# A 64-byte side load from sixteen rows, and the engine that waits for the last store, in a multiply-and-GELU kernel

## The chip, the cores and the metric

The kernel runs on one core of one Trainium2 chip. The metric is the device time of one execution in microseconds. Four executions of the kernel before took 119.97, 120.05, 120.23 and 120.64 us, with a median of 120.14 us. The profile shown here is that of the execution that took 119.97 us.

## The reference

Two float32 arrays `x` and `y` of 1024 x 4096 are multiplied element by element, and the tanh form of GELU is applied to the product.

```python
z = x * y
return (0.5 * z * (1 + np.tanh(np.sqrt(2 / np.pi) * (z + 0.044715 * z ** 3)))).astype(np.float32)
```

Each array has 16.78 MB. Two are read and one is written, so 50.33 MB cross between HBM and the on-chip memory (SBUF) in any version that reads and writes each element once.

## The kernel before

The arrays are seen as flat and cut into three pieces. A piece spans a range of columns of a picture of 128 partitions by 32768 columns: columns 0 to 1280 (640 KB in all), 1280 to 17664 (8 MB) and 17664 to 32768 (7552 KB). Inside a piece, each partition's columns are one contiguous run in HBM, and the partitions follow one another. A row below is one partition's part of a piece: 5 KB, 64 KB or 59 KB. Here the pieces are called the first, the second and the third.

All of `x` has a place in SBUF (`xs`), and the results are written over it. `y` has a smaller buffer (`ys`, 20440 columns), so its third and first pieces go where the second was, after parts of that have been used. `Y_LOADS` lists the pieces of `y` in the order of their loading, second, third, first, with their places in `ys`; `Y_FREE` says how many multiplications must be done before each load may be issued (0, 3 and 4).

All loads and stores are issued by SyncE (SP in the profile), in an order written out by hand:

1. `x` first piece and `x` second piece. `_hoist` moves these two issues ahead of the barrier among the engines with which the program begins.
2. After the barrier, `y` second piece and `x` third piece.
3. `y` third piece, after three multiplications, and `y` first piece, after four.
4. The three stores (line 113), second, third, first, each after the GELU of its columns (line 112).

VectorE multiplies (line 96) in steps of 4096 columns for the second piece, of 2048 and 768 for the third, and of 1280 for the first. ScalarE (ACT) applies GELU to each step (line 104) once `sem_mul` says that it is multiplied. At the end SyncE waits for the first two stores (line 115) and clears the semaphores but one (line 118). ScalarE waits for the last store and takes that semaphore back to zero (line 119):

```python
nc.sync.sem_clear(range(nums[0], nums[-1] + 1))
nc.scalar.wait_ge(sem_o[-1], 16).then_inc(sem_o[-1], -16)
```

ScalarE issues no transfer in this version. Line 59 is the closing of the tile scheduler, in which the engines pass two more rounds of the barrier.

Of the kernel before, what the change touches and what calls it, by code (L numbers as in the profile page):

```python
# [1 line left out]

# [4 lines left out]


F32 = mybir.dt.float32
GELU = mybir.ActivationFunctionType.Gelu_apprx_tanh  # L10

PIECES = [(0, 1280), (1280, 17664), (17664, 32768)]

Y_LOADS = [(1280, 17664, 4056), (17664, 32768, 0), (0, 1280, 15104)]

Y_FREE = [0, 3, 4]

STEPS = [[4096] * 4, [2048] * 7 + [768], [1280]]  # L20
STORES = [(1280, 17664), (17664, 32768), (0, 1280)]
Y_BUF = 20440


def _hoist(nc, issued):

    here = nc.cur_bb.bb.instructions
    first = nc.main_func.blocks[0].instructions
    for ins in issued:
        del here[next(k for k, i in enumerate(here) if i is ins or i.name == ins.name)]  # L30
    engine = issued[0].engine
    at = next(
        k
        for k, i in enumerate(first)
        if i.engine == engine and type(i).__name__ == "InstDrain"
    )
    first[at:at] = issued


@with_exitstack  # L40
def kernel(
    ctx: ExitStack,
    tc: tile.TileContext,
    x: bass.AP,
    y: bass.AP,
    out: bass.AP,
):
    nc = tc.nc
    P = nc.NUM_PARTITIONS

    def columns(t, a, b):

        flat = t.flatten_outer_dims().rearrange("r c -> (r c)")
        pa, pb = next(q for q in PIECES if q[0] <= a and b <= q[1])
        return flat[P * pa : P * pb].rearrange("(p c) -> p c", p=P)[:, a - pa : b - pa]


    tc.close()
    tc.compile()  # L59

    xs = nc.alloc_sbuf_tensor("xs", [P, PIECES[-1][1]], F32).ap()
    ys = nc.alloc_sbuf_tensor("ys", [P, Y_BUF], F32).ap()
    sem_x = [nc.alloc_semaphore(f"sem_x{i}") for i in range(len(PIECES))]
    sem_y = [nc.alloc_semaphore(f"sem_y{i}") for i in range(len(Y_LOADS))]
    sem_mul = nc.alloc_semaphore("sem_mul")
    sem_act = nc.alloc_semaphore("sem_act")
    sem_o = [nc.alloc_semaphore(f"sem_o{i}") for i in range(len(STORES))]

    def load_x(i):
        a, b = PIECES[i]  # L70
        return nc.sync.dma_start(out=xs[:, a:b], in_=columns(x, a, b)).then_inc(sem_x[i], 16)

    def load_y(i):
        a, b, r = Y_LOADS[i]
        return nc.sync.dma_start(
            out=ys[:, r : r + b - a], in_=columns(y, a, b)
        ).then_inc(sem_y[i], 16)

    _hoist(nc, [load_x(0).ins, load_x(1).ins])
    load_y(0)  # L80
    load_x(2)
    for i in range(1, len(Y_LOADS)):
        if Y_FREE[i]:
            nc.sync.wait_ge(sem_mul, Y_FREE[i])
        load_y(i)

    n = 0
    done = {}
    for i, (a, b, r) in enumerate(Y_LOADS):
        for j, (xa, xb) in enumerate(PIECES):  # L90
            if xa <= a < xb:
                nc.vector.wait_ge(sem_x[j], 16)
        nc.vector.wait_ge(sem_y[i], 16)  # L93
        c = a
        for w in STEPS[i]:
            nc.vector.tensor_mul(  # L96
                out=xs[:, c : c + w],
                in0=xs[:, c : c + w],
                in1=ys[:, r + c - a : r + c - a + w],
            ).then_inc(sem_mul, 1)  # L100
            n += 1
            done[c + w] = n
            nc.scalar.wait_ge(sem_mul, n)
            nc.scalar.activation(  # L104
                out=xs[:, c : c + w], in_=xs[:, c : c + w], func=GELU
            ).then_inc(sem_act, 1)
            c += w

    for i, (a, b) in enumerate(STORES):
        if i == 0:  # L110
            nc.sync.wait_ge(sem_y[-2], 16)
        nc.sync.wait_ge(sem_act, done[b])
        nc.sync.dma_start(out=columns(out, a, b), in_=xs[:, a:b]).then_inc(sem_o[i], 16)
    for i in range(len(STORES) - 1):
        nc.sync.wait_ge(sem_o[i], 16)
    nums = sorted(s.num for s in [*sem_x, *sem_y, *sem_o[:-1], sem_mul, sem_act])
    assert nums == list(range(nums[0], nums[-1] + 1))
    nc.sync.sem_clear(range(nums[0], nums[-1] + 1))
    nc.scalar.wait_ge(sem_o[-1], 16).then_inc(sem_o[-1], -16)


# [1 line left out]
_INS = ['x', 'y']  # L123
_OUTS = [((1024, 4096), 'float32')]


# [23 lines left out]
```

## Time and profile before

| What | Value |
|---|---|
| Time, median of four executions | 120.14 us (119.97 to 120.64) |
| Time of the profiled execution | 119.97 us |
| Its span, from the first to the last instruction of the program | 118.5 us |
| Time outside the span | about 1.5 us |
| Bytes moved, mean rate over the span | 50.33 MB, 425 GB/s |
| VectorE busy | 35.2 us (30% of the span) |
| ScalarE busy | 31.0 us (26%) |
| Share of the 16 DMA engines taken by packets | 98.8% |

The span begins with the first issue of a transfer on SyncE and ends with ScalarE's wait for the last store. The profile names an engine's queue of instructions with a q: SPq is SyncE issuing or waiting. An issue has a start, a length (the time SyncE spends on it), and a time to landing, counted from its start until the last of its bytes is reported. A landing in the span is the sum of the two. The table of windows gives busy time and transfers in stretches of the span that the reader of the trace chooses.

### The profile page before, as it was taken

The page shows a single profiled execution, that of the slowest core. Times are in us where ns is not written, and L with a number is a line of the kernel's source. Part 1 is how long each engine was busy: PE and PEld are TensorE (multiplying, and loading weights), DVE is VectorE, ACT ScalarE, POOL GpSimd, SP SyncE. Part 2 cuts the span into 40 slices and gives each one's busy share as a digit, 9 for nine tenths or more (in the row PEclk, how much of TensorE's full clock was granted, in tenths as well). Part 3 has the DMA queues.
Part 4 walks back from the last instruction along what each step waited for, and adds up shares of the span by engine and source line. Part 5 has one row for each costly group of instructions (what it writes and reads, how often), then busy time and mean ns, then how long its engine had stood idle before and what let it go on. Part 6 is the DMA issues. An engine that isn't in the chain of part 4 may idle for free.

```text
span 118.5 us, 82 instructions
## 1 busy us (share of the span) xinstructions
DVE 35.2 (30%) x13; ACT 31.0 (26%) x14; POOL 0.2 (0%) x4
## 2 busy tenths in 40 slices
DVE  0000000000000069999920000059999940000000
ACT  3000000000000001977974000006998990000000
POOL 0000000000000000000000000000000000000000
DMA  7988899888988897797797798798899887977975
GB/s 260 669 354 354 354 620 443 354 354 376 686 354 354 354 653 326 326 653 326 326 632 347 326 632 347 326 575 354 354 553 509 354 354 326 653 326 326 653 326 221
DMA packets 1296, 50.33 MB, mean 425 GB/s; under 512 B 144, under 2 KB 144, under 8 KB 528
## 3 DMA queue, kind: packets, MB, share of 16 engines
q1 hardware_dynamic: 1296, 50.33, 98.8%
HBM read 33.55 MB, written 16.78 MB: 425 GB/s over the span
## 4 chain that ended last, share of the span: by engine, by line
DMA 53%; DVE 24%; ACT 3%; issue 1%; DVEq 0%
DMA ys<-in_y_dram 53%; DVE xs L96 24%; ACT xs L104 3%; DVEq L93 0%
## 5 line engine op out<-in xcount | busy, mean ns | idle before, releaser
L96 DVE TENSOR_TENSOR xs<-xs,ys 128x2048 f32<-128x2048 f32 (+3 forms) x13 | 35.2, 2777 | 60.9 <-DMA ys<-in_y_dram 60.9
L104 ACT ACTIVATE xs<-xs 128x2048 f32<-128x2048 f32 (+3 forms) x13 | 29.7, 2301 | 64.7 <-DVE xs L96 64.7
L104 ACT ACT_TABLE_LOAD x1 | 1.3, 1283 | 1.9 <-PEq L59 1.9
L134 POOL MEMSET const-bfloat16-1.0<- 128x1 bf16 x1 | 0.1, 101 | 0.0
L134 POOL MEMSET const-uint8-127<- 128x1 uint8 x1 | 0.1, 101 | 0.0
L134 POOL MEMSET const-float32-0.0<- 128x1 f32 x1 | 0.1, 98 | 0.2 <-issue 0.2
L134 POOL MEMSET const-float32-1.0<- 128x1 f32 x1 | 0.1, 98 | 0.0
## 6 DMA issues: line engine op xcount, KB each, us to landing
xs<-in_x_dram SPq DMA_DIRECT2D x1, 7552.0 KB, 58.1
ys<-in_y_dram SPq DMA_DIRECT2D x1, 7552.0 KB, 22.5
out_dram<-xs SPq DMA_DIRECT2D x1, 7552.0 KB, 20.4
xs<-in_x_dram SPq DMA_DIRECT2D x1, 640.0 KB, 3.6
ys<-in_y_dram SPq DMA_DIRECT2D x1, 640.0 KB, 19.7
out_dram<-xs SPq DMA_DIRECT2D x1, 640.0 KB, 20.8
xs<-in_x_dram SPq DMA_DIRECT2D x1, 22.7
ys<-in_y_dram SPq DMA_DIRECT2D x1, 40.5
```

The source lines that it names most:

```text
L96: nc.vector.tensor_mul(out=xs[:, c : c + w], in0=xs[:, c : c + w], in1=ys[:, r + c - a : r + c - a + w],).then_inc(sem_mul, 1)
L104: nc.scalar.activation(out=xs[:, c : c + w], in_=xs[:, c : c + w], func=GELU).then_inc(sem_act, 1)
L134: nc = _bacc.Bacc("TRN2", target_bir_lowering=False, num_devices=1)
```

## The change

There are two edits.

The first adds a small load, called `touch`. ScalarE issues it, ahead of the first barrier. It reads 16 columns (64 B) of every eighth row of the second piece of `x`, sixteen rows in all, and writes them into `ys[:16, :16]`. These columns of `ys` are not used by the second piece of `y`; the third piece of `y` is loaded over them later. Nothing computes with the bytes. The load has a semaphore of its own, `sem_t`, and SyncE waits for it between the issue of the third piece of `x` and that of the third piece of `y`. `sem_t` is added to the range that is cleared at the end.

The second edit moves the wait for the last store from ScalarE to SyncE, behind SyncE's clearing of the other semaphores.

```diff
+    sem_t = nc.alloc_semaphore("sem_t")
...
+    a = PIECES[1][0]
+    touch = nc.scalar.dma_start(out=ys[:16, :16], in_=columns(x, a, a + 16)[:: P // 16, :]).then_inc(sem_t, 16)
+    _hoist(nc, [touch.ins])
     _hoist(nc, [load_x(0).ins, load_x(1).ins])
     load_y(0)
     load_x(2)
+    nc.sync.wait_ge(sem_t, 16)
     for i in range(1, len(Y_LOADS)):
...
-    nums = sorted(s.num for s in [*sem_x, *sem_y, *sem_o[:-1], sem_mul, sem_act])
+    nums = sorted(s.num for s in [sem_t, *sem_x, *sem_y, *sem_o[:-1], sem_mul, sem_act])
     assert nums == list(range(nums[0], nums[-1] + 1))
     nc.sync.sem_clear(range(nums[0], nums[-1] + 1))
-    nc.scalar.wait_ge(sem_o[-1], 16).then_inc(sem_o[-1], -16)
+    nc.sync.wait_ge(sem_o[-1], 16).then_inc(sem_o[-1], -16)
```

On every engine the other instructions stand in the same order as before.

## The prediction

> **What bounds the kernel now.** I read the page's queue line first, then its table of issues, then a table of windows cut at the landings, and last the waits of SyncE.
>
> ```profile
> DVE 35.2 (30%) x13; ACT 31.0 (26%) x14; POOL 0.2 (0%) x4
> q1 hardware_dynamic: 1296, 50.33, 98.8%
> DMA 53%; DVE 24%; ACT 3%; issue 1%; DVEq 0%
> ```
>
> Packets take 98.8% of the 16 DMA engines' time, and no compute engine is busy for a third of the span. The chain (third line) credits VectorE with 24%, but that is the order in which the last store was released; the queue stayed full meanwhile. So the end is set by the transfers, back to back from the first to the last, and an edit counts only if it starts the stream later, opens a hole in it, lengthens it, or lengthens what follows it.
>
> ```profile
> 0.00 0.38 SPq L71 DMA_DIRECT2D xs<-in_x_dram  x1
> 0.43 0.42 SPq L71 DMA_DIRECT2D xs<-in_x_dram  x1
> xs<-in_x_dram SPq DMA_DIRECT2D x1, 640.0 KB, 3.6
> xs<-in_x_dram SPq DMA_DIRECT2D x1, 22.7
> ```
>
> These are two rows of the timeline (start, length) and two of the issue table (size, time to landing). The first x piece is issued at 0.00 and lands at 3.6; the second at 0.43 and lands at 0.43 + 22.7 = 23.1. Doing the same for every issue gives the cuts of this table of windows; its first two columns are the stretch and its length.
>
> ```profile
> 0.00:3.63 3.63, 0.00 (x0) 1.28 (x1) 0.20 (x4) 1.00 1.23 469
> 3.63:23.10 19.47, 0.00 (x0) 0.00 (x0) 0.00 (x0) 1.00 1.00 431
> 23.10:42.45 19.35, 0.00 (x0) 0.00 (x0) 0.00 (x0) 1.00 0.99 429
> 78.20:79.74 1.54, 1.45 (x1) 0.00 (x0) 0.00 (x0) 1.00 2.14 910
> 79.74:99.10 19.36, 16.33 (x9) 15.26 (x9) 0.00 (x0) 1.00 0.99 429
> ```
>
> The rows are: x first piece, x second, y second, y first, store of the second. I use their lengths only (the last two columns, DMA share and GB/s, jump in a short stretch). Two comparisons matter. The second piece is 8 MB in three of the rows: x took 19.47 us, y 19.35, its store 19.36. So beside its equals the second x piece has lost only 0.11 to 0.12 us, and that is all that the small load can give back there. The first piece of 640 KB took 3.63 us at the start and 1.54 in the stream, for y: a start from nothing costs 2.09 us. A further window, 0.50 to 1.00, shows 0 GB/s, and 1.00 to 1.50 the first 174, so about 1.0 us of that is the way from issue to first packet, and 1.09 us is slow first rows and landing.
>
> **The small load, on its engine.** ScalarE gains one issue before the first barrier. SyncE's issues last 0.33 to 0.53 us, the nearest rows. ScalarE's other work there is a barrier drain at 0.1 us; SyncE reaches the barrier only after its two hoisted issues (0.85 us) and its drain at 0.9. If ScalarE issues from about 0.1, it is done by 0.1 + 0.53 = 0.63 and is not last at the barrier: cost 0. Without that cover the barrier would be late by the issue's length, and with it the y issue at 1.91. That too is covered: the y bytes are wanted only at 23.1. ScalarE's table load (1.92, 1.28 us) is wanted at 47.01, when its first GELU starts. So a late barrier costs nothing up to some 20 us.
>
> **The small load, in the transfers.** It adds 1 KB, sixteen packets of 64 B, probably one on each DMA engine, and 16 semaphore increments. The nearest row is the 640 KB piece in the stream: 1.54 us for 128 rows on 16 engines, so 8 rows on each at 0.19 us. A 64 B packet costs its engine between 0 (it fits into the slow first rows) and 0.19. I take half, 0.10, since the streaming row carries 80 times the bytes, but this packet is the first of its kind, and the first rows here are slow. The issue could also delay that of the first x piece, if the two cannot be served together: 0 to 0.42 us, from the length of SyncE's second hoisted issue. I take 0, since SyncE starts first and its own first issue is over at 0.38, where ScalarE has hardly begun.
>
> The Trainium skill has a rule that speaks against the edit: by "DMA: Bandwidth & Descriptors", section "Issuing engines are not separate DMA queues", transfers issued from several engines interleave on the same 16 DMA engines, so that a second issuer saves issue time alone; and its section "Measured (HBM→SBUF, 128 partitions, SWDGE, issued from GpSimd)" puts 4 KB at 0.68 us of transfer. If all of that stood ahead of the first x piece, an estimate by the page would be 119.97 + 0.68 = 120.65 us in the profiled execution. The page's figure is for another way of issuing, and no row here shows a transfer of this size, so it is no end of my range.
>
> **What it may give.** It reads from sixteen rows of the second x piece about two microseconds before that piece's turn. If that piece's deficit is the price of a first access, up to 0.11 us comes back. Against this stands the row of y: its second piece is just as untouched at 23.1 and shows no such loss. The stores' row agrees with y. So the 0.11 may as well be left from the disturbed start. The bounds are -0.11 and 0; I take -0.05, halfway.
>
> **The new wait on SyncE.** Behind `wait_ge(sem_t)` are queued the third and first pieces of y, and then the stores. The wait starts when the third x piece is issued, 2.29 + 0.53 = 2.82 us. The touch would land near the first x piece, at 3.6.
>
> ```profile
> 55.68 4.66 SPq L75 DMA_DIRECT2D ys<-in_y_dram  x2
> SPq L75 <- DVE xs L96: 56.8, 2, 52.8
> ```
>
> The next issue behind it is at 55.68 in the timeline, after 52.8 us of waiting for the third multiplication, as SyncE's waits say. A touch that lands at 3.6, or at 20, is hidden. Cost 0, cover some 50 us. The third y piece is stored over the touched columns after that wait, so no transfer is moved.
>
> **The last wait.** Before, SyncE waits for the second store at 116.9 and clears at 117.0; ScalarE's wait ends the span at 118.5. After, SyncE clears at the same point and then waits, so the clear stays hidden under the last store's 1.5 us, and one more semaphore in the range adds nothing. The wait is one instruction of 17 ns on either engine. What differs is what follows it outside the span, 119.97 - 118.5 = 1.5 us that no view of this trace divides by engine. The nearest row is a round of the barrier at the start:
>
> ```profile
> SPq L59 <- PEq L59: 0.5, 2, 0.3
> ```
>
> SyncE waits twice there, 0.3 us the longest. If the end is a round of the same kind, a late SyncE in place of a late ScalarE can shift it by up to one round, 0.3 us either way. Nothing excludes either sign; I take 0.
>
> **The sum.** 119.97 + 0.10 (packets) - 0.05 (second x piece) + 0 (issue, barrier, wait on `sem_t`) + 0 (last wait) = 120.02 us. The median of the four runs is 0.17 above the profiled one, so the forecast is 120.19, given as 120.2. A difference of 0.5%, 0.60 us, is about what a measurement of this kernel can tell from no change: below 119.54 is faster, above 120.74 slower. My terms taken together at their ends, -0.11 - 0.3 = -0.41 and +0.19 + 0.42 + 0.3 = +0.91, give 119.73 to 121.05.
>
> **Rivals.** *The touch pays the first transfer's start, and the first x piece queues behind it* (slower). The place is the first 3.6 us. The price is anything up to the 1.09 us that the 640 KB piece loses there beside its equal, on top of the way to the first packet; it decides the verdict once over half of it, 0.60 us, comes on top of what the first piece pays already. Then the first landing moves from 3.6 to between 4.2 and 4.7 and the time is 120.7 to 121.2. For it: every DMA engine would carry the small packet, and nothing in the stream can make up a late start. Against it: SyncE issues first, and two cold reads may wait side by side. Chance 0.26.
>
> *The touch and the moved wait both help* (faster). The deficit of 0.11 goes, the end gains 0.3, and the first piece itself finds a warmer path, gaining up to half of its 1.09: 120.14 - 0.11 - 0.3 - 0.55 = 119.2. Less than a gain of 0.2 in the first piece leaves it inside 0.60. For it: the first rows are slow. Against it: the touch reads other rows than the first piece's, and is issued later. Chance 0.12.
>
> *The touch warms nothing*, because what the second x piece loses is not a first access: 120.14 + 0.10 = 120.24, inside the forecast's case, which has 0.62 in all.
>
> **The numbers.** Faster 0.12, same 0.62, slower 0.26. For the range I take 119.6 to 121.0: it holds the forecast's case, from its low end of 119.73 and a little into the faster rival, and most of the slower one. Left out are about 0.10 below and 0.08 above.
>
> **What would show it.** Right: the first x piece still lands at 3.6 to 3.8 and the second between 23.0 and 23.2; stages of 8 MB at 19.35; SyncE's issue at 55.68 moves by no more than that; SyncE's last wait ends the span at 118.4 to 118.7; 1.5 us, give or take 0.3, remain outside. Wrong: a first landing after 4.2; a second x piece that gains more than 0.11; a hole in a later stage; or a time outside the span that differs by more than 0.3 us, for which the ScalarE queue or the place of the last wait would have to answer.

## The result: 0.15% less time, from the end of the program

The changed kernel takes 119.78 us (median of 46 runs, 119.67 to 121.12); beside it, the kernel before took 119.98 us (76 runs, 119.74 to 120.64). The ratio is 0.9985, with a 95% interval of 0.9979 to 0.9991. That is 0.18 us less. It is inside the 0.5% that the prediction called no change, and clear of no change all the same, thanks to the number of runs. The forecast was 0.05 us more than before. So the time lies in the stated range, and the direction was the other one.

The profiled execution after took 119.81 us, with the same span of 118.5 us as before. So 1.3 us instead of 1.5 stand outside the span. Over the 47 runs after whose span is listed, time less span has a mean of 1.34 us. For the kernel before it was 1.51, 1.49 and 1.52 in the three groups of runs in which it was measured beside the experiments. (Spans are listed to 0.1 us; the means smooth that.)

The page after, first the engines, then the queues, then the chain:

```profile
DVE 35.2 (30%) x13; ACT 31.0 (26%) x14; POOL 0.2 (0%) x4
q1 hardware_dynamic: 1296, 50.33, 98.6%
q10 hardware_dynamic: 32, 0.00, 0.0%
DMA 53%; DVE 24%; ACT 3%; issue 1%; DVEq 0%; SPq 0%
```

New are q10, and `SPq` at 0% in the chain (a wait at line 89 that is now an instruction of its own). q10 is ScalarE's queue: 32 packets, the 16 of the touch and their 16 semaphore increments. A share that prints as 0.0% is below 0.05% of 16 engines' 118.5 us, which is 0.95 us over all of them, or less than 0.06 us on each.

The timeline at the start after:

```profile
0.12 0.38 ACTq L81 DMA_DIRECT2D ys<-in_x_dram  x1
0.42 0.42 SPq L72 DMA_DIRECT2D xs<-in_x_dram  x1
1.91 0.33 SPq L76 DMA_DIRECT2D ys<-in_y_dram  x1
1.91 1.28 ACT L109 ACT_TABLE_LOAD   x1 [1.91 <-PEq L59]
```

Two rows of its issue table (size, time to landing):

```profile
xs<-in_x_dram SPq DMA_DIRECT2D x1, 640.0 KB, 3.5
ys<-in_x_dram ACTq DMA_DIRECT2D x1, 1.0 KB, 3.0
```

ScalarE's issue lasts 0.38 us and is over at 0.50. The first issue behind the barrier stands at 1.91, as before. The touch lands at 0.12 + 3.0 = 3.1, and the first x piece at 3.5 instead of 3.6.

The windows after, cut at the landings as in the prediction:

```profile
0.00:3.53 3.53, 0.00 (x0) 1.28 (x1) 0.20 (x4) 1.00 1.21 483
3.53:23.19 19.66, 0.00 (x0) 0.00 (x0) 0.00 (x0) 1.00 0.99 427
23.19:42.53 19.34, 0.00 (x0) 0.00 (x0) 0.00 (x0) 1.00 0.99 430
78.20:79.77 1.57, 1.47 (x1) 0.00 (x0) 0.00 (x0) 1.00 2.03 864
79.77:99.14 19.37, 16.30 (x9) 15.26 (x9) 0.00 (x0) 1.00 0.99 429
```

The second x piece, the one whose rows were touched, now takes 19.66 us instead of 19.47. The y piece and the store of the same size take 19.34 and 19.37. So the second row is longer, not shorter; the first row is 0.10 shorter, and both together end at 23.19 instead of 23.10. Where one transfer ends and the next begins varies by itself: in six profiles without the touch, with the same loads up to there, the first x piece landed between 3.38 and 3.63 us and the second took 19.45 to 19.75 us. Inside the span there is no gain to be found.

Two of SyncE's waits after:

```profile
SPq L89 <- DVE xs L101: 52.9, 1, 52.9
SPq L124 <- SPq L124: 1.4, 1, 1.4
```

The last instruction of the span, from the trace's answers on its line, before and after (duration in ns, start in us):

```profile
L119 ACTq EVENT_SEMAPHORE  x1: 17/17/17, 118.5 to 118.5; - x1
L124 SPq EVENT_SEMAPHORE  x1: 17/17/17, 118.5 to 118.5; - x1
```

Line 124 is the wait that moved. It lasts 1.4 us behind the clearing and ends the span at 118.5, as ScalarE's did. The releaser is given as its own line, presumably since the wait also takes the semaphore back.

### The profile page after: what moved, and what is told of

Read it like the earlier page. It is cut to its first block, busy times and chain, and to the rows that moved or that the text cites. A ratio compares the mean times of both kernels' runs of the same rounds, so it can differ in the third digit from the quotient of the medians.

```text
span 118.5 us, 84 instructions
## 1 busy us (share of the span) xinstructions
DVE 35.2 (30%) x13; ACT 31.0 (26%) x14; POOL 0.2 (0%) x4
## 4 chain that ended last, share of the span: by engine, by line
DMA 53%; DVE 24%; ACT 3%; issue 1%; DVEq 0%; SPq 0%
DMA ys<-in_y_dram 53%; DVE xs L101 24%; ACT xs L109 3%; DVEq L98 0%; SPq L89 0%
```

## The experiments

Two theories stood against each other. By the end theory, the gain lies behind the last instruction and comes from the engine that waits last. By the touch theory, it lies in the first 23 us and comes from the touch. Ratios are to the kernel before on the same chip, with 95% intervals.

### The last wait alone

```diff
-    nc.scalar.wait_ge(sem_o[-1], 16).then_inc(sem_o[-1], -16)
+    nc.sync.wait_ge(sem_o[-1], 16).then_inc(sem_o[-1], -16)
```

> The second edit alone: before, with the last wait on SyncE and no touch. End theory (the gain stands outside the span and comes from which engine waits last): ratio 0.9986 to before (0.16 us less), span unchanged at 118.5, time outside the span 1.34 instead of 1.50. Touch theory (the gain stands in the first 23 us and comes from the touch): ratio 1.000, 1.50 outside.

Measured: 119.74 us against 119.92, ratio 0.9983 (0.9975 to 0.9992); 1.34 us outside the span against 1.51, with the mean span 118.42 on both sides. The end theory holds: the second edit alone gives the whole gain.

### The touch alone

```diff
 (of the kernel after)
-    nc.sync.wait_ge(sem_o[-1], 16).then_inc(sem_o[-1], -16)
+    nc.scalar.wait_ge(sem_o[-1], 16).then_inc(sem_o[-1], -16)
```

> The first edit alone: the touch, with the last wait left on ScalarE. End theory: ratio 0.9995 to 1.0005, 1.50 us outside the span. Touch theory: ratio 0.9985, span shorter by 0.18 us, 1.50 outside.

Measured: 119.91 us against 119.92, ratio 0.9999 (0.9991 to 1.0008); 1.50 us outside. The touch neither gives nor costs anything that these runs can tell, which is 0.1 us either way. The second x piece landed at 23.11 us in this profile. With the kernel after it was 23.19 and, in a second profile, 23.04. Without the touch, six profiles with the same loads up to there gave 23.10, 23.10, 23.13, 23.05, 23.11 and 23.07.

### The last wait on the other three engines

In each, line 119 of the kernel before names another engine (`nc.vector`, `nc.tensor`, `nc.gpsimd` in place of `nc.scalar`), and there is no touch.

> Before, with the last wait on VectorE and no touch. If the barrier behind the program passes the engines in a fixed turn (TensorE, ScalarE, GpSimd, VectorE, SyncE, and back), as the spacing of the barrier's semaphore events in the trace of before suggests, then VectorE as the last saves two hops of about 0.04 us: 1.42 us outside the span, ratio 0.9993. If SyncE alone is special (its queue of transfers, say), VectorE gives 1.50 outside and ratio 1.000.

> Before, with the last wait on TensorE and no touch. By the fixed turn, TensorE stands before ScalarE: one hop of 0.03 to 0.04 us more, 1.54 us outside the span, ratio 1.0003; its slower handling of a semaphore (51 ns against 17) may add 0.03. If SyncE alone is special: 1.50 outside, ratio 1.000.

> Before, with the last wait on GpSimd and no touch; the fifth engine of the row. Fixed turn (measured so far outside the span: TensorE 1.66, ScalarE 1.51, VectorE 1.45, SyncE 1.34): GpSimd stands between ScalarE and VectorE, 1.47 to 1.49 us outside, ratio 0.9997. If what counts is only how fast an engine handles its own end, GpSimd may be anywhere, and more than 1.51 would speak against the turn.

Measured: VectorE 119.89 us, ratio 1.0000 (0.9991 to 1.0008); TensorE 120.15, 1.0016 (1.0008 to 1.0025); GpSimd 120.36, 1.0038 (1.0023 to 1.0052). Outside the span there were 1.45, 1.66 and 1.87 us. VectorE came near the fixed turn's figure outside the span; its ratio can't tell 0.9993 from 1. TensorE missed it by 0.12 and GpSimd by 0.4, so a turn alone is not enough.

The traces hold the rest. They record each count of the semaphore with which the engines meet behind the program, though not which engine made it. A pass has nine counts. Engines that stand ahead of the last one in the turn count early: TensorE, with nothing to do, at 2.1 us of the span in the kernel before. None counts early where TensorE has the last wait, one with ScalarE, two with GpSimd, three with VectorE and four with SyncE (at 2.13, 97.75, 97.79 and 97.83 us in the profile after). The next count comes only after the last wait, and then the others follow at 0.02 to 0.10 us from each other. Read from one profile of each kernel, in microseconds (a wait's start is that of its last record, which lasts 17 to 51 ns):

| Last wait on | Its start to the first count after it | Counts that follow | That first count to the last of the pass | Sum | Outside the span, mean |
|---|---|---|---|---|---|
| SyncE (after) | 0.161 | 4 | 0.165 | 0.326 | 1.34 |
| VectorE | 0.203 | 5 | 0.241 | 0.444 | 1.45 |
| ScalarE (before) | 0.165 | 7 | 0.324 | 0.489 | 1.51 |
| TensorE | 0.330 | 8 | 0.357 | 0.687 | 1.66 |
| GpSimd | 0.579 | 6 | 0.284 | 0.863 | 1.87 |

Two things decide, and their sum explains the last column, which is 0.97 to 1.02 us above it in every row. What follows the pass is the same everywhere: the first count of the next pass comes 0.79 us after its end in all five. One of the two is the engine's place in the turn: TensorE, ScalarE, GpSimd, VectorE, SyncE, and back to TensorE, as the numbers of counts ahead of the last wait and behind it show. The other is how long an engine takes from its last wait to its count, 0.16 us on ScalarE and SyncE and 0.58 on GpSimd. Why the engines differ in this, no run shows. SyncE is quick, and stands where the turn comes round: all others have counted already and only the way back is left.

The Trainium skill has such a barrier: "Runtime: NRT & Kernel Launch", section "The ~15µs preamble/postamble breakdown", gives the serpentine across the five engines, in its row on the barrier ahead of the kernel, 44 ns a hop over eight hops, about 355 ns. The whole pass here, with TensorE last, agrees: eight gaps in 0.357 us. By that page three hops fewer, from ScalarE to SyncE, would be an estimate of 0.13 us. The counts in these traces make it 0.324 - 0.165 = 0.16. The three gaps that go take 0.039, 0.044 and 0.023 us, 0.106 together. The other 0.054 comes from the gap at the turn, which is 0.098 us where ScalarE is last and 0.044 where SyncE itself is.

### Where the touch could have cost: issued first, and made larger

```diff
 (of the kernel after)
-    touch = nc.scalar.dma_start(out=ys[:16, :16], ...
-    _hoist(nc, [touch.ins])
-    _hoist(nc, [load_x(0).ins, load_x(1).ins])
+    touch = nc.sync.dma_start(out=ys[:16, :16], ...
+    _hoist(nc, [touch.ins, load_x(0).ins, load_x(1).ins])
```

> After, with the touch issued by SyncE ahead of the first x piece: the place that the slower rival gave it. By the length of an issue the stream starts 0.43 us later: ratio 0.9985 + 0.0036 = 1.002, first x landing at 3.9 to 4.1. If the slow first rows are a price that the first transfer pays once, the touch pays them and the first x piece is faster behind it: landing near 3.6, ratio about 0.999. By the slower rival, with the whole 1.09 us on top: landing 4.6, ratio 1.007.

Measured: 120.36 us, ratio 1.0032 (1.0020 to 1.0045), mean span 119.02 against 118.49. Its timeline:

```profile
0.00 0.39 SPq L81 DMA_DIRECT2D ys<-in_x_dram  x1
0.45 0.89 SPq L72 DMA_DIRECT2D xs<-in_x_dram  x2
```

Its issue table:

```profile
xs<-in_x_dram SPq DMA_DIRECT2D x1, 640.0 KB, 3.8
ys<-in_x_dram SPq DMA_DIRECT2D x1, 1.0 KB, 1.6
```

The first x piece is issued 0.45 us later and lands at 0.45 + 3.8 = 4.2. A touch that had landed at 1.6 has not made it faster. What is lost, 0.53 us of span, is the place of an issue on SyncE and 0.1 more. The slower rival's 1.09 us did not come even with the touch where that rival put it.

```diff
 (of the kernel after; the wide touch)
-    touch = nc.scalar.dma_start(out=ys[:16, :16], in_=columns(x, a, a + 16)[:: P // 16, :]) ...
+    touch = nc.scalar.dma_start(out=ys[:16, :4056], in_=columns(x, a, a + 4056)[:: P // 16, :]) ...
```

> After, with the touch 4056 columns wide (16,224 B in each of the sixteen rows) instead of 16. Price by bytes: a 64 KB row takes an engine 19.35 / 8 = 2.42 us in the stream, so 16,224 B cost 0.60 us and the time is 119.76 + 0.60 = 120.36, ratio 1.0036 to before; the second x piece's landing moves by the same. That would mean that the touch's 64 B cost 0.002 us on this scale and were never a risk. If the touched bytes, already read once, came back faster in the second x piece, it would be less, down to +0.3.

```diff
 (of the kernel after; the same bytes over all rows)
-    touch = nc.scalar.dma_start(out=ys[:16, :16], in_=columns(x, a, a + 16)[:: P // 16, :]) ...
+    touch = nc.scalar.dma_start(out=ys[:, :507], in_=columns(x, a, a + 507)) ...
```

> After, with a touch of 507 columns (2,028 B) of all 128 rows of the second x piece: the same 260 KB as the wide touch, which cost 2.6 us where its bytes were worth 0.60. If the loss there came from sixteen long rows going into sixteen partitions, this costs 0.60 by its bytes and a little for short rows: ratio 1.0035 to 1.005. If it came from two queues taking turns on an engine beside the first x piece, it costs 2 to 3 us again: ratio 1.015 to 1.022.

Measured: the wide touch 122.41 us, ratio 1.0204 (1.0190 to 1.0218); the spread one 120.70 us, 1.0062 (1.0049 to 1.0074). Mean spans rose by 2.6 and 0.95 us, where the bytes were worth 0.60. Both theories for the wide one missed low by far. Most of its loss goes when the same bytes are spread over 128 rows. The packet records show where it lay: the wide touch's sixteen packets took 1.29 us each in the mean, and the 48 rows of the first x piece that began after 2.7 us took 0.70 (median) instead of 0.20; beside the spread touch such rows stayed at 0.20. So two queues at work at once are not enough to cause it. The two touches differ in the length of the rows, in their number and in the partitions they go to, and no run parts these. The windows of the wide touch:

```profile
0.00:6.26 6.26, 0.00 (x0) 1.28 (x1) 0.20 (x4) 1.00 1.11 314
6.26:25.61 19.35, 0.00 (x0) 0.00 (x0) 0.00 (x0) 1.00 1.00 434
```

All of the loss stands in the first stage. The second x piece behind it takes 19.35 us, as long as its equals and less than the 19.45 to 19.75 of a second transfer without the touch. A quarter of the bytes of sixteen rows had been read a moment before. That this took the 0.1 us off is not shown: behind the spread touch, with as many bytes read, the piece took 19.63 us (from 4.43 to 24.06).

### Why the second transfer is longer than its equals

```diff
 (of the kernel with the last wait alone moved)
-    _hoist(nc, [load_x(0).ins, load_x(1).ins])
-    load_y(0)
+    _hoist(nc, [load_x(0).ins, load_y(0).ins])
+    load_x(1)
```

> The last wait on SyncE, no touch, and the second pieces of y and x in the other order: y's is issued second and x's third. If the 0.1 to 0.3 us by which the second transfer is longer than its equals belongs to the start of the stream, it now stands with y: y's stage 19.45 to 19.75, x's 19.35, ratio 0.9985 as with the last wait on SyncE alone. If it is the price of a first access to x's second piece, it goes with x to the third place.

Measured: 119.78 us, ratio 0.9986 (0.9977 to 0.9995). Its windows:

```profile
3.50:23.06 19.56, 0.00 (x0) 0.00 (x0) 0.00 (x0) 1.00 0.99 429
23.06:42.42 19.36, 0.00 (x0) 0.00 (x0) 0.00 (x0) 1.00 0.99 429
```

The first of the two rows is now y's and the second x's. The deficit has stayed with the second place in the stream, in this one profile. It belongs to the start, as the row of y had said, and not to x's rows.

### A try for more: the first store not held back

```diff
 (of the kernel with the last wait alone moved)
-        if i == 0:
-            nc.sync.wait_ge(sem_y[-2], 16)
```

> The last wait on SyncE, no touch, and without the wait for the third y piece ahead of the first store: a try for a better version. In the traces some DMA engines run dry for 0.1 to 0.3 us where the first store is issued only when that piece has landed. If the engine that ends last is one of those, up to 0.15 us comes off beyond the 0.16 of the last wait: ratio 0.997. If it is one that never ran dry, nothing: 0.9985. If stores queued beside the last loads disturb them: above 0.999.

Measured: 121.14 us, ratio 1.0093 (1.0079 to 1.0107), the third case, and far above its 0.999. The store is issued at 63.6 instead of 78.2, and the loads ahead of it on the same queue land later. The first row is from the kernel before, the other two from this run:

```profile
60.35:78.20 17.85, 0.00 (x0) 3.28 (x1) 0.00 (x0) 1.00 0.92 396
60.27:78.93 18.66, 0.00 (x0) 3.33 (x1) 0.00 (x0) 1.00 0.92 373
78.93:81.20 2.27, 2.18 (x1) 0.00 (x0) 0.00 (x0) 1.00 1.69 663
```

The third piece of y takes 18.66 us instead of 17.85, and its first piece 2.27 instead of 1.54. The wait that looked like a hole is worth over a microsecond.

### The changed kernel again

No edit.

> The kernel after, unchanged, beside the next two on one chip. By what the parts gave (last wait on SyncE 0.9983, touch 0.9999): 0.9983 to 0.9986, 1.34 us outside the span, span as before within 0.05.

Measured: 119.79 us, ratio 0.9983 (0.9974 to 0.9992), 1.33 us outside, mean span 118.47 as before. The parts add up. No version tried beats the kernel with the last wait alone moved (0.9983), which does without the touch.

## Why the prediction was wrong

What failed is the direction: 0.05 us more was forecast, and 0.18 less came, from a term that the sum had at nothing.

*The bound.* Right: the transfers set the end, and no step of compute moved it.

*The last wait.* This step failed. The text bounded it by a round of the starting barrier, 0.3 us either way, and said "Nothing excludes either sign; I take 0". It measured -0.17 us (1.51 to 1.34 outside the span), inside the bound and with a definite sign. The counts put 0.16 of it down to the shorter way round. The views of the profile do not divide the 1.5 us, but the events on the barrier's semaphore in the trace of before do: seven counts followed ScalarE's own, over 0.324 us. Read before the run, they would have said that an engine later in the turn gives some of that back. Which engine stands where they do not say; that took the traces of the other kernels.

*The touch's packets.* Mis-sized. Taken at 0.10 us, half of a 5 KB row; the queue line puts them below 0.06 on each engine, and the packet records of the trace have 8 to 11 ns for each of the sixteen. The row of a much larger packet was a bound, and no reason for its middle. The estimate of 120.65 us that stood beside the sum was missed too: the touch alone took 119.91.

*The second x piece.* Taken at -0.05 of a possible 0.11. That bound came from one profile; in the six without the touch the piece took 0.1 to 0.4 us more than 19.35, while its landing stayed within 23.05 to 23.13. The touch gave nothing back: the argument against, that y shows no deficit at its first access, was the right one, and the longer stage went to y when y was loaded second. With this and the packets, the touch's sum of +0.05 stands against a measured -0.01, within 0.1 either way.

*The issue on ScalarE and the wait on `sem_t`.* Right at 0 both: the issue is over at 0.50 us, and the touch landed over 52 us before SyncE's next issue. That issue now follows a wait instruction of its own, 17 ns at 55.7, and stands at 55.81 instead of 55.68, hidden under the third x piece, which lands at 60.4.

*The level.* The forecast stood on the median of four runs, 120.14; with 76 runs it is 119.98. Of the 0.41 us between 120.19 and 119.78, this is 0.16, the touch's terms are 0.05, and the fall of the median from 119.98 to 119.78 is 0.20.

*The rivals.* None came. The slower one's mechanism cost 0.53 us when brought about on purpose, by an issue more ahead of the stream. The faster one had the moved wait, at half its price, and no warmer path. That the touch warms nothing was put inside the forecast's case and is what the runs show.

## What to carry to other kernels

When a stream of transfers fills the span, look also behind the last instruction: which engine ends last was worth up to 0.5 us here (1.34 us with SyncE, 1.87 with GpSimd). The barrier's counts in the trace show beforehand how long the way round is, but not how late another engine would come to it: GpSimd was missed by 0.4 us. Before loading bytes ahead to warm a path, ask whether an equal transfer elsewhere in the stream, just as untouched, shows the loss at all. Where two edits come together, run each alone: here the one with all the new code gave nothing.

## What the runs showed of the hardware that was not expected

- The engines pass the closing barrier in a turn, 0.357 us for the whole of it, with SyncE at its far end, and differ in how fast they come to it: 0.16 us from the last wait on SyncE and ScalarE, 0.20 on VectorE, 0.33 on TensorE, 0.58 on GpSimd.
- The same touch was under way at once from SyncE and late from ScalarE: issued first on SyncE's queue, it landed in 1.6 us; on ScalarE's, 0.12 us behind SyncE's first issue, in 3.0 us. Its first packet then moved 2.0 us after the issue, where that of the first x piece moved after 1.0. Whether the engine, the second queue or the load already under way makes it late was not tried.
- A side load of 253.5 KB (the 260 KB above) beside the first transfer cost 2.6 us in sixteen rows and 0.95 in 128, where its bytes were worth 0.60.
- Stores that were queued behind loads on the same queue made the loads land late, by 0.8 and 0.7 us in two stages. What passes between them was not tried.
